# A hybrid diffusion trunk step in fp32: the second layer's up product by seven block products of 320 columns, and tokens in slabs without padding columns

## The chip, the core and the metric

The kernel runs on one core of a Trainium2 chip. The metric is the device time of the program in microseconds, the median of the runs; lower is better. The core has TensorE (PE, matmul), VectorE (DVE), ScalarE (ACT), GpSimd (POOL) and a queue of its own for DMA (SP). PEld is the loading of weights into TensorE, which overlaps its matmuls.

## The reference

One step of a trunk of two layers for 640 tokens: 128 context tokens and 512 latent ones, 1024 features. Per layer, cut to what matters:

```python
h = modulate(x, sh1, sc1)                       # RMS norm, scale, shift
proj = h @ p['w_in']                            # q, k, v, z, x/B/C, dt, two gates
attn = block_attention(q, k_all, v_all)
xbc = silu(dw_conv(xbc, conv_w, conv_b))        # 3 taps over tokens
ssd, h_final = ssd_branch(xbc, z, dt_raw, ...)  # scan in both directions
merged = sigmoid(ga) * (attn @ w_attn_o) + sigmoid(gs) * (ssd @ w_ssd_o)
x = x + g1 * (merged @ p['w_out'])
h = modulate(x, sh2, sc2)
u = dw_conv(h @ p['w_up'], p['ffn_conv_w'], p['ffn_conv_b'])   # 1024 -> 5632
u_val, u_gate = split(u, 2)
x = x + g2 * ((silu(u_gate) * u_val) @ p['w_down'])            # 2816 -> 1024
```

Everything is float32. The convolutions run over the tokens of one request, so context and latent tokens must not mix at their border.

## The kernel before

**Products in two parts.** A float32 operand is split into a high part (`wh` of the weights, `hT[0]` of the tokens, by a cast on ScalarE to fp32r) and a low part (`wl`, `hT[1]`, by `dve.tensor_sub` of the source and the high part). A product is three matmuls per block of 128 features: high by high, high by low, low by high. Weights come from DRAM into `wr` (two buffers of [128, 2048], 1 MB), and `wprep` makes `wh` and `wl` of them (three buffers each); `AHEAD = 2` units are recorded before the item that needs them.

**Feature-major products** (`feat_half`) have 128 weight columns stationary and tokens moving. They make x, B, C and dt of the input projection (25 feature blocks in each layer) and the up product (44 in each layer). The tokens lie with two columns of zeros between context and latent, 642 in all, and move in two parts of `HALF = (386, 256)` columns; one part is 8 blocks x 3 = 24 matmuls into one PSUM bank. `conv_in` brings it out twice on ScalarE (a copy into `raw`, the middle tap with its bias into `cc`), `conv_taps` adds the two outer taps on VectorE.

**Token-major products** (`tok_major`) have tokens stationary and 512 weight columns moving: 24 matmuls per tile of 128 tokens. The output projection (`w_out_item`) and the down product (`down_item`) are of this kind.

**The up stage.** `up_item(p, jl)` takes two weight units of 256 columns, one of the value half and one of the gate half: two feature blocks each, and two token parts, so 8 x 24 = 192 matmuls. After the convolution the gate block goes through `silu2` and the product with the value block and is split into `S["g", p]`. A layer has 11 items: four, then the down product of those 8 blocks in two items (`n`), four, down, three, down. The first item takes the first token parts of all four blocks ahead of the second parts, because the last tiles are still being normed: `w_out_item` with `n == 1` updates the five token tiles one by one and norms each (`norm_tile`, `norm_mod`), which splits it into `S["h2"]`, made by `new_hT`.

**What sets the order.** The program is recorded as operations on tiles (`Flow.record`) and then ordered by a list scheduler (`Flow.issue`) with costs of its own, ranks by class (`RANK`) and buffers granted in the order of asking. Each engine then runs its instructions strictly in that order. All are issued from one helper line, so rows of the profile tell by tile names what they are: `pf`, `pp`, `p`, `pq` are PSUM banks (`pf` three), `slab` holds tokens or gated blocks, `fw` the taps and biases of the up product's convolution, `tmp` the convolution's buffers (seven of class `f`, seven of class `d`).

## Time and profile before

| | us |
|---|---|
| median of 3 runs | 2858.25 (2858.05 to 2859.9) |
| span of the profiled execution | 2854.8 |
| TensorE busy | 2816.5 |
| VectorE busy | 2066.4 |
| ScalarE busy | 1291.9 |
| GpSimd busy | 90.5 |

The span runs from the first to the last instruction of the one execution that the hardware profiler recorded; 3.45 us separate it from the median. Busy times of one engine can overlap in themselves, since an instruction's recorded end lies behind the start of the next, so the pitch, from start to start, is read from the timeline. The second layer's up and down stage runs from 2384 us to the end.

### The profile page before, as it was taken

How to read it: one execution, taken by the hardware profiler on the slowest of the kernel's cores; microseconds unless marked ns; L12 is line 12 of the kernel's file. 1: busy time of each engine (PE TensorE's matmuls, PEld its weight loads, DVE VectorE, ACT ScalarE, POOL GpSimd, SP SyncE). 2: the span in 40 equal slices, each digit the busy share in tenths (PEclk: the TensorE clock that was granted, in tenths of full speed). 3: DMA queues.
4: the chain of work that ended last, by engine and by line, in shares of the span. 5: the costliest groups of instructions: out<-in, count | busy, mean ns of one | idle time of the engine just before them, and what ended most of it. 6: DMA issues, size and time to landing. Idle time of an engine off the chain costs nothing.

```text
span 2854.8 us, 41191 instructions
## 1 busy us (share of the span) xinstructions
PE 2816.5 (99%) x15620; PEld 2456.6 (86%) x15620; DVE 2066.4 (72%) x2851; ACT 1291.9 (45%) x2255; POOL 90.5 (3%) x408
## 2 busy tenths in 40 slices
PE   6999999999999999999999999999999999999999
PEld 4898997877788898998979989887887888989898
DVE  7878775987799599997677666598779456545554
ACT  6454654445353453452444645544454325524342
POOL 1200000000000000000011000000000000000000
PEclk9999999999999999999999999999999999999999
DMA  7343444677868546455352223457667553252423
GB/s 262 100 125 126 126 151 143 225 247 245 275 219 275 180 136 215 167 175 180 98 168 85 94 95 100 155 199 251 220 235 258 203 175 132 86 166 65 155 84 111
DMA packets 309679, 478.45 MB, mean 168 GB/s; under 512 B 19808, under 2 KB 139792, under 8 KB 304360
## 3 DMA queue, kind: packets, MB, share of 16 engines
q1 hardware_dynamic: 309480, 475.81, 50.0%
q8 instruction: 123, 2.02, 0.3%
q14 instruction: 76, 0.62, 0.1%
HBM read 384.08 MB, written 91.65 MB: 167 GB/s over the span
## 4 chain that ended last, share of the span: by engine, by line
PE 95%; DMA 3%; DVE 1%; ACT 1%; issue 0%; SPq 0%; POOL 0%; DVEq 0%; ACTq 0%
PE pf L178 79%; PE p L178 10%; PE pp L178 4%; PE pq L178 1%; DMA tmp<-in_state_ssd_dram 1%; DMA slab<-in_w_mod_dram 0%; DVE tmp L178 0%; DMA ga<-tmp 0%; DVE wl L178 0%; DMA tmp<-in_x_prompt_dram 0%; ACT tmp L178 0%; SPq L178 0%; DMA slab<-in_q_norm_dram 0%; DVE slab L178 0%; ACT wh L178 0%
## 5 line engine op out<-in xcount | busy, mean ns | idle before, releaser
L178 PE MATMUL pf<-wh,slab 128*128 128x512 f32 x3920 | 1268.3, 400 | 5.9 <-ACT slab L178 2.5
L178 PE MATMUL pf<-slab,wh 128*128 128x256 f32 (+1 forms) x4416 | 980.2, 311 | 3.4 <-DVE slab L178 1.9
L178 PEld LDWEIGHTS pf<-wh,slab 128*128 128x128 f32 x3920 | 733.1, 189 | 174.4 <-issue 7.3
L178 PE MATMUL pf<-wl,slab 128*128 128x512 f32 x1960 | 780.7, 398 | 0.0
L178 PEld LDWEIGHTS pf<-slab,wh 128*128 128x128 f32 x4416 | 741.8, 189 | 12.0 <-issue 5.7
L178 PE MATMUL pf<-slab,wl 128*128 128x256 f32 (+1 forms) x2208 | 685.1, 310 | 0.0
L178 DVE TENSOR_TENSOR wl<-wr,wh 128x2048 fp32r<-128x2048 f32 (+1 forms) x156 | 350.7, 2248 | 145.3 <-ACT wh L178 144.5
L178 PEld LDWEIGHTS pf<-wl,slab 128*128 128x128 f32 x1960 | 369.5, 189 | 86.6 <-issue 6.0
L178 ACT CAST wh<-wr 128x2048 fp32r<-128x2048 f32 (+1 forms) x156 | 293.0, 1879 | 320.7 <-PE pf L178 302.4
L178 PEld LDWEIGHTS pf<-slab,wl 128*128 128x128 f32 x2208 | 415.9, 188 | 3.0 <-issue 0.2
L178 DVE SCALAR_TENSOR_TENSOR tmp<-tmp,fw,tmp 128x642 f32<-128x642 f32 x176 | 155.5, 885 | 80.5 <-ACT tmp L178 66.3
L178 PE MATMUL p<-tmp,slab 128*128 128x64 f32 (+1 forms) x976 | 209.8, 336 | 0.3 <-DVE tmp L178 0.3
L178 ACT ACTIVATE tmp<-tmp 128x642 f32<-128x642 f32 (+2 forms) x176 | 120.9, 687 | 179.1 <-DVE tmp L178 145.5
L178 ACT ACTIVATE tmp<-pf,fw 128x386 f32<-128x386 f32 (+1 forms) x176 | 109.0, 620 | 175.4 <-PE pf L178 172.2
L178 DVE TENSOR_TENSOR tmp<-pf,tmp 128x512 f32<-128x512 f32 x100 | 68.3, 688 | 132.1 <-PE pf L178 131.8
L178 PEld LDWEIGHTS p<-tmp,slab 128*128 128x128 f32 x976 | 136.0, 190 | 16.2 <-ACT tmp L178 4.6
L178 ACT COPY tmp<-pf 128x256 f32<-128x256 f32 (+3 forms) x296 | 127.5, 431 | 44.1 <-PE pf L178 43.7
L178 DVE TENSOR_TENSOR slab<-tmp,slab 128x512 fp32r<-128x512 f32 (+4 forms) x182 | 109.0, 634 | 42.9 <-ACT slab L178 42.7
L178 DVE SCALAR_TENSOR_TENSOR macc<-tmp,cT,macc 128x512 f32<-128x512 f32 x196 | 137.7, 743 | 1.2 <-DMA tmp<-in_w_mod_dram 1.2
L178 DVE TENSOR_TENSOR tmp<-tmp,tmp 128x512 f32<-128x512 f32 (+3 forms) x190 | 133.7, 705 | 3.0 <-DMA tmp<-sz 0.6
L178 PEld LDWEIGHTS p<-cst,tmp 128*128 128x128 f32 (+2 forms) x750 | 92.3, 141 | 40.6 <-issue 16.1
L178 PE MATMUL p<-cst,tmp 128*128 128x128 f32 (+2 forms) x750 | 121.0, 276 | 5.1 <-DMA tmp<-in_state_ssd_dram 4.4
(131 smaller groups left out, 2564.3 us busy)
## 6 DMA issues: line engine op xcount, KB each, us to landing
wr<-in_w_in_dram SPq DMA_DIRECT2D x60, 1024.0 KB
wr<-in_w_up_dram SPq DMA_DIRECT2D x44, 1024.0 KB
slab<-row SPq DMA_DIRECT2D x40, 1024.0 KB
tmp<-in_w_mod_dram SPq DMA_DIRECT2D x116, 256.0 KB
tmp<-xres SPq DMA_DIRECT2D x85, 256.0 KB
wr<-in_w_down_dram SPq DMA_DIRECT2D x20, 1024.0 KB
tmp<-xs SPq DMA_DIRECT2D x72, 256.0 KB
xres<-tmp SPq DMA_DIRECT2D x70, 256.0 KB
```

The costliest lines, as they stand in the source:

```text
L178: self.ops.append((lane, lambda: call(*args, **kw), self._cost(lane, fn, outs, ins, kw), deps, touched, self.cls))
```

## The change

Four things are edited together.

1. **Up product of the second layer, all items but the first.** Of each weight unit (1024 x 256) the two feature blocks and the two halves of the 1024 inputs make four blocks `a11, a12, a21, a22` of 512 x 128; the tokens make four of 512 x 320. Their product is made by Winograd's form of Strassen's algorithm: seven block products of 12 matmuls of 320 columns (`product`), with sums of weights (`Sums`: s1 to s4, made in place in `wr`), sums of tokens (`Blocks.sums`: t1 to t4) and sums of products. Products accumulate on one another in a PSUM bank where they can; `win_unit` copies intermediate sums out between two accumulations. Of the last product of a unit (`rest`) the recording is put off into the next unit.
2. **No padding columns among the tokens.** `HALF = (256, 384)`; the context is tokens 0 to 127 at once, and `padded` puts the columns of a bank to their places when they leave it. `conv_bufs` clears the two border columns of `raw` and `cc` on GpSimd. The second layer's `S["h2"]` is a `Blocks`, in halves of 320.
3. **Slabs of one size.** One tag of four slabs for tokens instead of two tags of two; `NSLABD` 7 instead of 5. The decay tables of `dt_item` (`karr`) lie in one of these instead of in buffers of their own.
4. A rank `u` ahead of all others on ScalarE and VectorE for what empties PSUM in `win_unit`; a smaller scratch for GpSimd's DMA, which the kernel does not use.

```diff
-HALF = (386, 256)
-HOFF = (0, 386)
+HALF = (256, 384)
-NSLABD = 5
+NSLABD = 7
+WIN = (1,)
+TH = 320
...
-        "pe": {"m": 0, "d": 1, "f": 2}, "act": {"f": 0, "d": 1, "m": 2}, "dve": {"f": 0, "d": 1, "m": 2},
+        "pe": {"m": 0, "d": 1, "f": 2}, "act": {"u": -1, "f": 0, "d": 1, "m": 2},
+        "dve": {"u": -1, "f": 0, "d": 1, "m": 2},
...
+    class Blocks:
+        def __init__(self):
+            self.R = [slabd([P, 4, TOK]) for _ in range(2)]
+            self.X = {k: slab([P, 2, 4, TH], F32R) for k in ("11", "21", "22")}
+            self.X["12"] = slabd([P, 2, 4, TH], F32R)
...
+        def part(self, k, src=None):
+            x = self.X[k]
+            split(x[:, 0], x[:, 1], self.raw(k) if src is None else src)
+
+        def sums(self):
+            tr = slabd([P, 2, 4, TH])
+            for k in ("t1", "t2", "t3"):
+                self.X[k] = slabd([P, 2, 4, TH], F32R)
+            self.X["t4"] = slab([P, 2, 4, TH], F32R)
+            dve.tensor_sub(tr[:, 0], self.raw("11"), self.raw("12"))
+            self.part("t1", tr[:, 0])
+            dve.scalar_tensor_tensor(tr[:, 1], tr[:, 0], -1.0, self.raw("22"), ALU.mult, ALU.subtract)
+            self.part("t2", tr[:, 1])
+            t3, t4 = self.raw("12"), self.raw("21")
+            dve.tensor_sub(t3, self.raw("22"), t3)
+            self.part("t3", t3)
+            dve.scalar_tensor_tensor(t4, tr[:, 1], -1.0, t4, ALU.mult, ALU.subtract)
+            self.part("t4", t4)
...
+    class Sums:
+        def __init__(self, parts):
+            r, _ = wraw(parts, False)
+            v = r.rearrange("p (j k i c) -> p j k i c", j=2, k=4, i=2)
+            hl = [[flow.tile(wp, [P, 4, 4, P], F32R, n, nm(n), 3) for n in ("wh", "wl")] for _ in range(2)]
...
+            a11, a12, a21, a22 = v[:, 0, :, 0], v[:, 1, :, 0], v[:, 0, :, 1], v[:, 1, :, 1]
...
+            dve.tensor_add(s3, a11, a21)
+            put(0, 0, 2, v[:, :, :, 0])
+            dve.tensor_add(a21, a21, a22)
+            put(0, 2, 1, a21)
+            dve.tensor_add(a11, s3, a22)
+            put(0, 3, 1, a11)
+            dve.tensor_add(a12, a11, a12)
+            put(1, 0, 1, a12)
+            put(1, 1, 1, s3)
+            put(1, 2, 1, a22)
...
+    def product(ps, w, x, start):
+        wh, wl = w
+        for k in range(4):
+            for j, (w, b) in enumerate(((wh, 0), (wh, 1), (wl, 0))):
+                pe.matmul(
+                    ps, lhsT=w[:, k, :], rhs=x[:, b, k, :], start=start and k + j == 0, stop=k + j == 5,
+                    skip_group_check=not start,
+                )
...
+    def win_unit(W, X, bufs, taps, done):
...
+        product(a, W["a11"], X["11"], True)
+        now(act.copy, p1c, a)
+        product(c, W["s1"], X["t1"], True)
+        now(act.copy, p5c, c)
+        catch_up()
+        product(a, W["s2"], X["t2"], False)
+        now(act.copy, u2, a)
+        product(b, W["a12"], X["21"], True)
+        r0, c0 = bufs(0)
+        for src, dst in halves(r0):
+            now(dve.tensor_add, dst, p1c[:, src], b[:, src])
+        product(c, W["s4"], X["22"], False)
+        now(dve.tensor_add, r0[:, TH + 3:COLS + 1], u2, c)
+        product(a, W["s3"], X["t3"], False)
+        now(act.copy, u3, a)
+        conv(0, r0, c0)
+
+        def rest():
+            product(a, W["a22"], X["t4"], False)
+            r1, c1 = bufs(1)
+            dve.scalar_tensor_tensor(r1[:, TH + 3:COLS + 1], u3, -1.0, p5c, ALU.mult, ALU.subtract)
+            for src, dst in halves(r1):
+                now(act.mul, dst, a[:, src], -1.0)
+            conv(1, r1, c1)
+
+        behind.append(rest)
...
+        pool.memset(raw[:, P + 1:P + 3], 0.0)
+        pool.memset(cc[:, P:P + 2], 0.0)
...
-                    S["h2"] = new_hT()
+                    S["h2"] = Blocks() if l in WIN else new_hT()
...
+                        if l in WIN and i == 2:
+                            S["h2"].part("11")
+                            S["h2"].part("21")
+                if l in WIN and n == 1:
+                    S["h2"].part("12")
+                    S["h2"].part("22")
+                    S["h2"].sums()
...
-                add([w_feat(w_up, l, P * j, 256), w_feat(w_up, l, P * (NFF + j), 256)], up_item(p, jl))
+                us = [w_feat(w_up, l, P * j, 256), w_feat(w_up, l, P * (NFF + j), 256)]
+                if l in WIN and p + jl > 0:
+                    us = [lambda u=u: Sums(u) for u in us]
+                add(us, up_item(p, jl))
```

**Where instructions stand, TensorE, an up item of the second layer.** Before, at the step from a token part of 386 columns to the next of 256 (one feature block, `pf` the bank, `slab` the tokens):

```order
L178 MATMUL pf_3731<-slab_3653,wl_3702 128x386
L178 MATMUL pf_3731<-slab_3653,wh_3701 128x386
L178 MATMUL pf_3731<-slab_3655,wh_3701 128x386
L178 MATMUL pf_3731<-slab_3653,wl_3702 128x386
L178 MATMUL pf_3731<-slab_3653,wh_3701 128x386
L178 MATMUL pf_3731<-slab_3655,wh_3701 128x386
L178 MATMUL pf_3731<-slab_3653,wl_3702 128x386
L178 MATMUL pf_3732<-slab_3654,wh_3701 128x256
L178 MATMUL pf_3732<-slab_3656,wh_3701 128x256
```

Now, at the step from the first product of a unit (a11 by its tokens) to the second (s1 by the sum t1):

```order
L180 MATMUL pf_3765<-slab_3647,wl_3733 128x320
L180 MATMUL pf_3765<-slab_3647,wh_3732 128x320 x2
L180 MATMUL pf_3765<-slab_3647,wl_3733 128x320
L180 MATMUL pf_3765<-slab_3647,wh_3732 128x320 x2
L180 MATMUL pf_3765<-slab_3647,wl_3733 128x320
L180 MATMUL pf_3765<-slab_3647,wh_3732 128x320 x2
L180 MATMUL pf_3765<-slab_3647,wl_3733 128x320
L180 MATMUL pf_3766<-slab_3692,wh_3732 128x320 x2
L180 MATMUL pf_3766<-slab_3692,wl_3733 128x320
L180 MATMUL pf_3766<-slab_3692,wh_3732 128x320 x2
```

What moved: a bank is filled by 12 matmuls of 320 columns instead of 24, and the next product takes other weights of the same unit and other tokens.

**VectorE, the same items.** Before, one item's rows (`wl` a weight unit's low part, rows with `fw` the taps, the others gate, product and split):

```order
L178 TENSOR_TENSOR wl_3747<-wr_3745,wh_3746 128x2048
L178 SCALAR_TENSOR_TENSOR tmp_3738<-tmp_3737,fw_2252,tmp_3738 128x642 x2
L178 TENSOR_TENSOR wl_3750<-wr_3748,wh_3749 128x2048
L178 SCALAR_TENSOR_TENSOR tmp_3742<-tmp_3741,fw_2252,tmp_3742 128x642 x2
L178 SCALAR_TENSOR_TENSOR tmp_3742<-tmp_3741,tmp_3742 128x642
L178 SCALAR_TENSOR_TENSOR tmp_3752<-tmp_3751,fw_2252,tmp_3752 128x642
L178 TENSOR_TENSOR tmp_3742<-tmp_3742,tmp_3738 128x642
L178 SCALAR_TENSOR_TENSOR tmp_3752<-tmp_3751,fw_2252,tmp_3752 128x642
L178 TENSOR_TENSOR slab_3705<-tmp_3742,slab_3703 128x642
```

Now, a third of an item (`wr` rows are sums of weights in place, `wl` their low parts):

```order
L180 TENSOR_TENSOR wr_3731<-wr_3731 128x4x128
L180 TENSOR_TENSOR wl_3733<-wr_3731,wh_3732 128x512
L180 TENSOR_TENSOR wl_3735<-wr_3731,wh_3734 128x512
L180 SCALAR_TENSOR_TENSOR tmp_3750<-tmp_3749,fw_2248,tmp_3750 128x642
L180 TENSOR_TENSOR wl_3735<-wr_3731,wh_3734 128x512
L180 SCALAR_TENSOR_TENSOR tmp_3750<-tmp_3749,fw_2248,tmp_3750 128x642
L180 SCALAR_TENSOR_TENSOR tmp_3752<-tmp_3751,fw_2248,tmp_3752 128x642
L180 TENSOR_TENSOR tmp_3758<-wr_3753 128x512
L180 SCALAR_TENSOR_TENSOR tmp_3752<-tmp_3751,fw_2248,tmp_3752 128x642
L180 TENSOR_TENSOR wr_3753<-wr_3753 128x4x128
L180 TENSOR_TENSOR wl_3755<-wr_3753,wh_3754 128x1024
L180 SCALAR_TENSOR_TENSOR tmp_3752<-tmp_3751,tmp_3752 128x642
```

What moved: the low part of a unit of 2048 columns has become ten instructions, and they stand between the taps.

**VectorE, where the second layer's last token tile is modulated** (`TENSOR_SCALAR`, four blocks). Before, what follows is the tile's split, then the first item's taps:

```order
L178 TENSOR_SCALAR tmp_3691<-p_3592_3696,sm_3627 128x128 x4
L178 TENSOR_TENSOR slab_3656<-tmp_3692,slab_3654 128x4x128
L178 TENSOR_TENSOR slab_3656<-tmp_3691,slab_3654 128x4x128
L178 SCALAR_TENSOR_TENSOR tmp_3708<-tmp_3707,fw_2252,tmp_3708 128x642 x2
L178 SCALAR_TENSOR_TENSOR tmp_3711<-tmp_3710,fw_2252,tmp_3711 128x642 x2
L178 TENSOR_TENSOR wl_3725<-wr_3723,wh_3724 128x2048
```

Now the low parts and sums of whole blocks of 1280 columns follow (`slab_3645` and `slab_3646` are the tokens unsplit), then the rest of a weight unit:

```order
L180 TENSOR_SCALAR slab_3646<-p_3586_3690,sm_3619 128x128 x4
L180 TENSOR_TENSOR slab_3691<-slab_3645 128x1280
L180 TENSOR_TENSOR slab_3650<-slab_3645,slab_3650 128x1280
L180 TENSOR_TENSOR slab_3649<-slab_3646,slab_3649 128x1280
L180 TENSOR_TENSOR slab_3692<-slab_3691,slab_3692 128x1280
L180 SCALAR_TENSOR_TENSOR slab_3691<-slab_3691,slab_3646 128x1280
L180 TENSOR_TENSOR slab_3645<-slab_3646,slab_3645 128x4x320
L180 SCALAR_TENSOR_TENSOR slab_3646<-slab_3691,slab_3646 128x4x320
L180 TENSOR_TENSOR slab_3693<-slab_3691,slab_3693 128x1280
L180 TENSOR_TENSOR slab_3694<-slab_3645,slab_3694 128x1280
L180 TENSOR_TENSOR slab_3695<-slab_3646,slab_3695 128x1280
L180 TENSOR_TENSOR wl_3703<-wr_3699,wh_3702 128x512
```

What moved: ten instructions of 1280 columns stand between the last tile and the taps of the first item, which come third after the last row shown.

## Rows read from the trace of the kernel before

**Rows 1.** Page, part 1: busy us, share of the span, instructions.
```profile
PE 2816.5 (99%) x15620; PEld 2456.6 (86%) x15620; DVE 2066.4 (72%) x2851; ACT 1291.9 (45%) x2255; POOL 90.5 (3%) x408
```

**Rows 2.** Stretches: length, busy us of PE, PEld, DVE, ACT, POOL, clock, DMA.
```profile
2440.28:2468.23 27.95, 27.95 (x194) 27.95 (x193) 16.31 (x16) 14.07 (x23) 0.51 (x8) 1.00 0.23 76
1048.00:1076.00 28.00, 28.00 (x190) 27.46 (x190) 26.57 (x35) 14.69 (x24) 0.71 (x8) 1.00 0.46 150
```

**Rows 3.** Timeline of PE, an up item: start us, us, what, xcount, idle before.
```profile
2400.39 0.34 PE L178 MATMUL pf<-slab,wl 128*128 128x386 f32 x1
...
2406.23 0.34 PE L178 MATMUL pf<-slab,wl 128*128 128x386 f32 x1
...
2406.64 0.28 PE L178 MATMUL pf<-slab,wl 128*128 128x256 f32 x1
...
2407.66 0.28 PE L178 MATMUL pf<-slab,wl 128*128 128x256 f32 x1
```

**Rows 4.** Timeline of PE where attention's 320 columns stand.
```profile
160.38 1.04 PE L178 MATMUL pp<-slab,slab 128*128 128x320 f32 x6
161.26 0.33 PE L178 MATMUL pf<-slab,wh 128*128 128x386 f32 x1
```

**Rows 5.** Groups of DVE by shape: xcount, busy us, mean ns of one.
```profile
L178 DVE SCALAR_TENSOR_TENSOR tmp<-tmp,fw,tmp 128x642 f32<-128x642 f32 x176 | 155.5, 885 | 80.5 <-ACT tmp L178 66.3 <-issue 6.6 <-POOL tmp L178 2.5
...
L178 DVE TENSOR_TENSOR slab<-tmp,slab 128x512 fp32r<-128x512 f32 x100 | 64.8, 686 | 27.7 <-ACT slab L178 27.6
...
L178 DVE TENSOR_TENSOR tmp<-tmp,slab 128x128 f32<-128x128 f32 x64 | 14.3, 285 | 0.0
...
L178 DVE SCALAR_TENSOR_TENSOR tmp<-tmp,tmp 128x320 f32<-128x320 f32 x18 | 8.8, 491 | 0.5
L178 DVE TENSOR_TENSOR wl<-wr,wh 128x1024 fp32r<-128x1024 f32 x6 | 7.3, 1224 | 6.7 <-ACT wh L178 6.7
```

**Rows 6.** Timeline of DVE, second layer, without a wait between.
```profile
2385.35 1.29 DVE L178 TENSOR_TENSOR slab<-tmp,slab 128x512 fp32r<-128x512 f32 x2
...
2418.82 0.82 DVE L178 SCALAR_TENSOR_TENSOR tmp<-tmp,tmp 128x642 f32<-128x642 f32 x1
2419.55 0.88 DVE L178 SCALAR_TENSOR_TENSOR tmp<-tmp,fw,tmp 128x642 f32<-128x642 f32 x1
2420.35 0.82 DVE L178 TENSOR_TENSOR tmp<-tmp,tmp 128x642 f32<-128x642 f32 x1
```

**Rows 7.** Timeline of PE, second layer, output projection into up.
```profile
2382.82 0.39 PE L178 MATMUL pf<-wl,slab 128*128 128x512 f32 x1
...
2383.51 0.39 PE L178 MATMUL pf<-wl,slab 128*128 128x512 f32 x1
2384.64 0.59 PE L178 MATMUL pf<-slab,wh 128*128 128x386 f32 x2 [0.74 <-ACT slab L178]
2386.18 0.42 PE L178 MATMUL pf<-slab,wh 128*128 128x386 f32 x1 [0.94 <-DVE slab L178]
...
2387.27 0.53 PE L178 MATMUL pf<-slab,wl 128*128 128x386 f32 x1
...
2388.23 0.53 PE L178 MATMUL pf<-slab,wl 128*128 128x386 f32 x1
```

**Rows 8.** The same step of the first layer, PE, then DVE.
```profile
979.80 0.59 PE L178 MATMUL pf<-slab,wh 128*128 128x386 f32 x2 [0.73 <-ACT slab L178]
981.34 0.41 PE L178 MATMUL pf<-slab,wh 128*128 128x386 f32 x1 [0.95 <-DVE slab L178]
981.59 0.34 PE L178 MATMUL pf<-slab,wl 128*128 128x386 f32 x1
...
982.13 0.34 PE L178 MATMUL pf<-slab,wl 128*128 128x386 f32 x1
...
991.35 1.06 PE L178 MATMUL p<-cst,tmp 128*128 128x128 f32 x8
...
994.21 1.29 DVE L178 TENSOR_TENSOR slab<-tmp,slab 128x512 fp32r<-128x512 f32 x2 [0.38 <-ACT slab L178]
```

More of the change, by code (lines that the diff above doesn't have):

```diff
@@ L366, in nm, with slab @@
         return f"{s}_{uid[0]}"
-    def slab(h, shape, dt=F32):
-        return flow.tile(slabs, shape, dt, f"slab{h}", nm("slab"), 2)
+    def slab(shape, dt=F32):
+        return flow.tile(slabs, shape, dt, "slab", nm("slab"), 4)
     def slabd(shape, dt=F32):
@@ new lines, in product, with halves, catch_up @@
+    def product(ps, w, x, start):
[6 more added lines that the diff above has]
+                )
+    def halves(raw):
+        return (slice(0, P), raw[:, 1:P + 1]), (slice(P, TH), raw[:, P + 3:TH + 3])
+    behind = []
+    def catch_up():
+        while behind:
+            behind.pop(0)()
@@ new lines, in win_unit, with now, conv @@
+    def win_unit(W, X, bufs, taps, done):
+        W, X = W.w, X.X
+        a, c = psf()[:, 0:TH], psf()[:, 0:TH]
+        flow.cls = "d"
+        ta, tb = cv((P, 2, TH)), cv((P, 2, TH))
+        b = flow.tile(p1, [P, 512], F32, "p1", nm("p1"), 2)[:, 0:TH]
+        flow.cls = "f"
+        p1c, p5c, u2, u3 = ta[:, 0], ta[:, 1], tb[:, 0], tb[:, 1]
+        def now(fn, *args, **kw):
+            flow.cls = "u"
+            fn(*args, **kw)
+            flow.cls = "f"
+        def conv(k, raw, cc):
+            w0, w1, w2, bias = taps(k)
+            act.activation(cc, raw[:, 1:COLS + 1], AF.Identity, scale=w1, bias=bias)
+            conv_taps(raw, cc, w0, w2)
+            done(k)
+        product(a, W["a11"], X["11"], True)
[22 more added lines that the diff above has]
+        behind.append(rest)
@@ L597, in norm_mod @@
                 dve.tensor_scalar(h[:, k, :], src[:, k, :], sc, sh, ALU.mult, ALU.add)
-        b, o = part(i)
-        ks = slice(4 * n, 4 * n + 4)
-        split(hT[0][b][:, ks, o:o + P], hT[1][b][:, ks, o:o + P], h)
+        if not isinstance(hT, Blocks):
+            o = slice(i * P, (i + 1) * P)
+            split(hT[0][n][:, :, o], hT[1][n][:, :, o], h)
     def norm_tile(x0, x1, t, i, modT, hT):
@@ L972, in arr @@
                 return t2()[:, 0:n]
+            kar = slabd([P, 5, NT, 64])
+            kn = iter(range(5))
             def karr(tag):
-                return keep([P, NT, 64], F32, tag)
+                return kar[:, next(kn)]
             def fl(t):
@@ L1345, in half, with gated, new @@
                     raw, cc = bufs[a, s]
[L1346 to L1347 removed]
+                    if l in WIN:
+                        ps = feat_half(ws[s], 256, a * P, S["h2"].cols(h), TH)
+                        if h == 0:
+                            for src, dst in halves(raw):
+                                act.copy(dst, ps[:, src])
+                        else:
+                            act.copy(raw[:, TH + 3:COLS + 1], ps)
+                            act.activation(
+                                cc, raw[:, 1:COLS + 1], AF.Identity, scale=f[:, 1, s, j:j + 1], bias=f[:, 3, s, j:j + 1]
+                            )
+                    else:
+                        ps = feat_half(ws[s], 256, a * P, part_h(S["h2"], h), HALF[h])
+                        conv_in(raw, cc, ps, h, f[:, 1, s, j:j + 1], f[:, 3, s, j:j + 1])
                     if h == 1:
                         conv_taps(raw, cc, f[:, 0, s, j:j + 1], f[:, 2, s, j:j + 1])
[L1350 removed]
+                        gated(a, s)
+                def gated(a, s):
+                    if s == 1:
                         k = jl + a
[L1352 removed]
+                        (raw, cc), cu = bufs[a, 1], bufs[a, 0][1]
                         silu2(raw, cc)
                         dve.tensor_mul(cc, cc, cu)
[L1355 removed]
+                        split(gs[0][k // 4][:, k % 4, :], gs[1][k // 4][:, k % 4, :], cc)
+                def new(a, s):
+                    bufs[a, s] = conv_bufs()
+                    return bufs[a, s]
+                if isinstance(ws[0], Sums):
+                    for s in range(2):
+                        win_unit(
+                            ws[s], S["h2"], lambda a, s=s: new(a, s),
+                            lambda a, s=s: [f[:, r, s, j0 + a:j0 + a + 1] for r in range(4)],
+                            lambda a, s=s: gated(a, s),
+                        )
+                    return
                 if p == 0 and jl == 0:
@@ L1369, in fn @@
             def fn(ws):
+                catch_up()
                 g = gate_bc(l, 1, n)
```

74 lines of the change are left out of this document (46 added, 28 removed).

## Prediction

> **What bounds the kernel now.** I read the busy times first. TensorE is busy for 2816.5 us of a span of 2854.8 us, and all matmuls together leave it 38 us idle [rows 1]. So the time is the length of TensorE's stream, and an edit gains what it takes out of that stream, less what TensorE then waits. VectorE is second with 2066.4 us, but that is a mean over stages. The stage that the change rebuilds is the second layer's up product, so I read one of its items next, in the table of stretches: 27.95 us, TensorE busy all of it, VectorE 16.31 us, ScalarE 14.07 us [rows 2]. The engine that can take the bound from TensorE there is VectorE, which gets the new sums.
>
> **The price of a matmul.** TensorE's busy time overlaps, so I take start to start. Eleven times three matmuls of 386 columns go from 2400.39 to 2406.23, which is 0.177 us each; nine of 256 columns go from 2406.64 to 2407.66, 0.113 us each [rows 3]. 96 x (0.177 + 0.113) = 27.8 us, the item of [rows 2]. Six of 320 columns start at 160.38 and the next matmul at 161.26, 0.147 us each [rows 4]; by columns between 256 and 386 it would be 0.145. I take 0.146.
>
> **Term 1, seven products for eight.** Before, a pair of feature blocks (one weight unit) is two blocks of 24 matmuls of 386 and 24 of 256 columns, half an item: 13.98 us. After, it is seven products of 12 matmuls of 320 columns, as the order of TensorE shows, 84 x 0.146 = 12.26 us. That is 1.72 us for each of 20 units, **-34.3 us** (-32.6 at 0.147, -36.0 at 0.145). The first item of the second layer stays a product by eight; its 192 matmuls of 320 columns take 28.0 us, as before.
>
> **Term 2, no padding columns.** 94 feature blocks (25 of the input projection in each layer, 44 of the first layer's up) have 24 matmuls each of 384 instead of 386 columns: 2,256. The trace has no 384. From the nearest row, 386, in proportion, one saves 0.0009 us, together 2 us. On the line through 256 (0.113) and 512 columns (0.230: the third of one three starts at 2382.82 and that of the next at 2383.51 [rows 7]), 384 would take 0.1715 and one saves 0.0055, together 12 us. I take the nearest, **-2 us**, and keep 12 for the range.
>
> **Term 3, what VectorE has to do.** Its price is start to start too: two of 512 columns last 1.29 us together, where one lasts 0.686 [rows 5, 6]; one of 0.82 us is followed after 0.73, one of 0.88 after 0.80 [rows 6]. So an instruction in a full queue costs its duration less 0.086 us. With the durations of [rows 5] this makes 0.60 for 512 columns, 1.14 for 1024, 0.80 for a tap of the convolution, 0.74 for 642 columns without a per-partition scalar [rows 6], 0.405 for 320, 0.20 for 128; between these 0.27 for 192, and beyond them, at 1.053 ns a column, 1.41 for 1280 and 2.2 for 2048.
>
> A weight unit before was one subtraction of 2048 columns, 2.2 us. Now it is four additions of 512, one low part of 1024 and five of 512: 9 x 0.60 + 1.14 = 6.5 us. Joining the products adds 0.20 + 0.27 + 2 x 0.405 = 1.3 us a unit. Eight taps (6.4) and six instructions of 642 columns (4.4) an item stay. So an item asks VectorE for 2 x 7.8 + 10.8 = 26.4 us, beside 24.5 us of TensorE: VectorE no longer hides behind the item, though 26.4 is still below the 27.95 of before. It can only work ahead and behind: the down products between are long and ask it for little.
>
> So I count VectorE's rows in the order of the changed kernel over each of the three stretches, up products and the head of the down products that needs them, against TensorE's. After the last token tile is modulated the first stretch has 147 instructions: 10 of 1280 (the token sums), 49 of 512, 5 of 1024, 32 taps, 24 of 642, 12 of 320, 6 of 192, 6 of 128, 3 of 2048, together 106.9 us, and 1.7 us before they begin. TensorE has 628 matmuls of 320 columns and 63 of 512 at 0.230 before it needs the last gated tile: 91.7 + 14.5 = 106.2 us. The second stretch: 161 instructions, 106.1 us and 1.5 before, against 98.1 + 14.5 = 112.6. The third: 117 instructions, 77.3 and 1.5, against 73.6 + 10.4 = 84.0. With no gap on VectorE TensorE would wait 2.4 us in all. Gaps there will be: nearly every low part waits for ScalarE's high part, and the joins wait for TensorE while everything behind them on VectorE stands. How dense can VectorE be while TensorE is fed? In an up item of the first layer it was busy 26.57 of 28.00 us, 95%, and TensorE lost nothing [rows 2], but a part of that was modulation work that could wait. At 95% the three stretches cost 8.0 + 0.6 + 0 = 8.6 us, at 90% 14.3 + 6.8 + 3.4 = 24.5 us. I take 93%: 10.4 + 3.0 + 0.6 = **+14 us**.
>
> **Term 4, the first layer's step into up.** The first halves now need two tiles instead of three, so the waits of 0.73 and 0.95 us for the third [rows 8] go. But four first halves last 4 x 24 x 0.113 = 10.9 us instead of 17.0, and the last tile's split ends only at 994.21 + 1.29 = 995.5 [rows 8]. TensorE leaves the output projection at about 979.1; with 10.9, two groups of transposes (0.8 each) and eight small matmuls (0.23) it is done at 993.4 and then waits some 1.5 us, with a chance of a slower clock: after 1.7 us of such waits in the second layer the 386-column matmuls start 0.32 us apart from 2387.27 to 2388.23 instead of 0.177 [rows 7], which is the 1.2 GHz level and costs 1 to 2 us in the few that it lasts, while after the same waits in the first layer three take 0.54 us from 981.59 on [rows 8]. **+1 us**, from -1 to +4.
>
> At no cost I enter the additional memsets of the two padding columns (POOL is busy 90.5 us in all [rows 1]), ScalarE (14.07 us of an item [rows 2]; the casts grow from 2048 to 3584 columns a unit, still under 24.5), and the two more slabs, since a freer order elsewhere can only win back idle time, of which little is left [rows 1].
>
> **Sum.** -34.3 - 2 + 14 + 1 = -21.3 us. The profiled execution spans 2854.8 us and the median is 2858.25, 3.45 us around it; the sum goes on both alike: a span of 2833.5, a median of **2837 us**.
>
> [...] The rows of a full queue [rows 6] show an instruction of VectorE starting 0.086 us before the one ahead has ended. [...]
>
> **Rivals.** (a) VectorE keeps up, waits of 3 us or less, and 384 columns run nearer the line: -36 - 12 + 2.4 = about -46, 2812; with 2 us for the padding 2824. For it speaks that the second and third stretch have 5 us in hand, against it that the first has none. (b) Full durations: 0.086 us more for 147, 161 and 117 instructions makes 119.5, 119.9 and 87.4 us, waits of 15.0 + 8.8 + 4.9 = 28.7 us and -6.6 in all, 2852. For it speaks that instructions which wait for their own predecessor do not overlap, against it the queue without waits [rows 6]. (c) **Slower**: VectorE becomes the bound of the up items. Its queue is strictly in order, and a join that waits for a product holds the weights of the next unit behind it, for which TensorE then waits. It decides from a density of 87%: there the waits are 18.4 + 10.9 + 6.4 = 35.7 us and eat the gain. At 84% they are 22.8 + 15.2 + 9.5 = 47.5 us, +12, 2870. For it speaks that an item of before, with idle time to spare, filled VectorE to 58% only [rows 2] and so proves nothing of 90; against it the 95% of the first layer. (d) The change does not do what it says: the order has seven products of 12 in each unit, so this is left at 0.01.
>
> **How the numbers follow.** My forecast, waits of 3 to 25 us (2825 to 2848): 0.50. (a), below 2825: 0.14. (b), 2848 to 2856: 0.13. Between (b) and (c), 2856 to 2864: 0.06. (c), above 2864: 0.16, and (d) 0.01. About 0.2% (5.7 us) is what a measurement of this kernel can tell from no change: faster than 2852.5 is the forecast, (a) and a small part of (b), 0.68; within it 0.15; slower 0.17. The range leaves out the far end of (a) and the worse half of (c), a density below 85% (43.4 us of waits, +8): 2814 to 2866.
>
> **What would show it.** TensorE's instructions fall by 240 and its 320-column matmuls start 0.145 to 0.147 us apart. VectorE's busy time rises by about 20 x 5.6 us and 11 for the token sums, to 2190 us. An item of seven products takes 24.5 us where it is not held. TensorE's waits for the low parts of weights and for the joins stand in the first of the three stretches above all, 14 us in the three, and VectorE is busy over 90% there. 384-column matmuls 0.172 us apart would say that term 2 was too small; up items of over 27 us with VectorE near 85% and TensorE waiting for it would say (c); full queues of VectorE without overlap, (b).

## The result, and the profile after

The changed kernel takes 2875.27 us (median of 4 runs, 2872.91 to 2878.35) against 2859.07 of the kernel before in the same comparison: a ratio of 1.0062, 95% interval 1.0049 to 1.0074. It is slower by 16 us, where 21 us of gain were predicted. The profiled execution spans 2871.1 us, 16.3 more than before.

Part 1 of the page of the changed kernel, busy us of each engine (before: [rows 1]):

```profile
PE 2804.9 (98%) x15380; PEld 2426.5 (85%) x15380; DVE 2184.4 (76%) x3113; ACT 1331.4 (46%) x2353; POOL 111.2 (4%) x672
```

TensorE has 240 instructions fewer and is busy 11.6 us less. VectorE's busy time rose to 2184.4, as forecast (2190). The edit does what it says, and yet the span grew, so TensorE idles more, somewhere. To find where, I cut both timelines of TensorE at the same steps of the program: the first matmul of 512 columns after the convolutions, the first of an up product, and so on.

| stage (start read from TensorE's timeline) | before | after | difference |
|---|---|---|---|
| until the first layer's z product | 402.7 | 402.4 | -0.3 |
| first layer: z, gates, SSD, output projection | 577.1 | 603.4 | **+26.3** |
| first layer: up and down | 549.2 | 552.2 | +3.0 |
| second layer: input projection, attention | 291.3 | 291.0 | -0.3 |
| second layer: z, gates, SSD, output projection | 564.3 | 566.1 | +1.8 |
| second layer: up and down | 470.2 | 456.0 | **-14.2** |

The last row is the place of the change, and it gains. The second is a stage in which nothing was rebuilt, a layer ahead of the block products, and it loses more. Its start in the timeline of TensorE before (its end there, 979.80, is in [rows 8]), then its two ends in the changed kernel's:

```profile
402.72 0.48 PE L178 MATMUL pf<-wh,slab 128*128 128x512 f32 x1
```

```profile
402.38 0.48 PE L180 MATMUL pf<-wh,slab 128*128 128x512 f32 x1
...
1005.82 0.40 PE L180 MATMUL pf<-slab,wh 128*128 128x256 f32 x2
```

In that stage two things share TensorE: token-major products (16 items of 5 x 24 matmuls of 512 columns) and SSD, 20 chunks (four groups of heads, five token tiles each), each a chain over VectorE, ScalarE and TensorE. Of the 1920 matmuls of the items, 1440 need nothing of SSD's last group. The last two items with SSD's output need it, tile by tile, and the two of the output projection come behind them. Both kernels at the end of SSD, in stretches (length, busy us of PE, PEld, DVE, ACT, POOL, granted clock, DMA), first before:

```profile
800.00:840.00 40.00, 40.00 (x205) 32.29 (x203) 37.69 (x53) 20.65 (x41) 0.00 (x0) 1.00 0.58 202
840.00:880.00 40.00, 40.00 (x193) 32.96 (x192) 36.03 (x56) 16.12 (x29) 1.37 (x2) 1.00 0.83 285
880.00:920.00 40.00, 40.00 (x192) 32.86 (x191) 35.85 (x53) 12.65 (x17) 0.23 (x2) 1.00 0.77 244
```

and after:

```profile
800.00:840.00 40.00, 39.86 (x184) 31.42 (x184) 29.65 (x40) 20.57 (x40) 0.00 (x0) 1.00 0.75 276
840.00:880.00 40.00, 35.58 (x162) 25.77 (x162) 39.03 (x57) 20.62 (x39) 0.00 (x0) 0.90 0.58 191
880.00:920.00 40.00, 32.88 (x149) 26.23 (x148) 34.77 (x54) 12.69 (x21) 1.38 (x2) 0.89 0.74 245
```

Before, TensorE is full to the last. After, from 840 to 880 VectorE is full (39.03 of 40) and TensorE runs beside it with 162 matmuls where it had 193, then with 149 where it had 192. The output of the last SSD chunk (eight heads, `p`, 64 columns, 16 matmuls), before at 847.86 us:

```profile
847.86 1.90 PE L178 MATMUL p<-tmp,slab 128*128 128x64 f32 x16
```

and after, that of the last two chunks (872.77 and 882.06 us), with what stands around it on TensorE:

```profile
872.77 2.00 PE L180 MATMUL p<-tmp,slab 128*128 128x64 f32 x16 [0.72 <-ACT tmp L180]
874.58 0.48 PE L180 MATMUL pp<-tmp,slab 128*128 128x512 f32 x1
876.40 1.22 PE L180 MATMUL pp<-tmp,slab 128*128 128x512 f32 x2 [1.34 <-DVE tmp L180]
877.42 1.05 PE L180 MATMUL pf<-wh,slab 128*128 128x512 f32 x2
878.27 0.63 PE L180 MATMUL pf<-wl,slab 128*128 128x512 f32 x1
...
882.06 1.90 PE L180 MATMUL p<-tmp,slab 128*128 128x64 f32 x16
...
893.86 0.40 PE L180 MATMUL pf<-wl,slab 128*128 128x512 f32 x1
901.33 1.22 PE L180 MATMUL pf<-wh,slab 128*128 128x512 f32 x2 [7.07 <-DVE tmp L180]
```

The last output comes 34 us later. By 860 us the 1440 matmuls, and the 24 of the first token tile that SSD had finished, were used up, so the last chunks ran with little beside them, each step waiting for the one before on another engine. Two matmuls of 512 columns take 0.85 us (877.42 to 878.27) instead of 0.46: the lower level of the clock, after TensorE had waited again and again. Then a token-major product waits 7.07 us. The engine named, VectorE, holds the join that frees a bank, but does modulation (`macc`) meanwhile; what it stands behind is on ScalarE's row, the load of SSD's last output (`y`) from DRAM, and on its own, the load of the join's other operand (`pb`), which the DMA queue issues right after that of `y` (895.47 and 895.94 us). The modulation lasts until 899.35 itself, so these rows do not tell what an earlier load alone would have saved. VectorE, then ScalarE:

```profile
891.98 7.37 DVE L180 SCALAR_TENSOR_TENSOR macc<-tmp,cT,macc 128x512 f32<-128x512 f32 x11
...
900.58 0.69 DVE L180 TENSOR_TENSOR tmp<-pf,tmp 128x512 f32<-128x512 f32 x1 [0.39 <-DMA tmp<-pb]
901.19 0.74 DVE L180 SCALAR_TENSOR_TENSOR macc<-tmp,cT,macc 128x512 f32<-128x512 f32 x1
```

```profile
898.85 0.62 ACT L180 CAST slab<-tmp 128x512 fp32r<-128x512 f32 x1 [8.30 <-DMA tmp<-y]
```

None of this is new work: the stage has the same 1920 matmuls in another order. TensorE's waits in it sum to 15.0 us, against 3.8 before, and by the granted clock of the last two stretches (0.90 and 0.89) some 8 us more went to the lower level; the rest of the 26 us is spread. Whether the order is the cause is for the experiments.

### The profile page after: what moved, and what is told of

Same layout as the page of the kernel before. It is cut to its first block, busy times and chain, and to the rows that moved or that the text cites. A ratio compares the mean times of both kernels' runs of the same rounds, so it can differ in the third digit from the quotient of the medians.

```text
span 2871.1 us, 41287 instructions
## 1 busy us (share of the span) xinstructions
PE 2804.9 (98%) x15380; PEld 2426.5 (85%) x15380; DVE 2184.4 (76%) x3113; ACT 1331.4 (46%) x2353; POOL 111.2 (4%) x672
## 5 line engine op out<-in xcount | busy, mean ns | idle before, releaser
L180 PE MATMUL pf<-slab,wh 128*128 128x256 f32 (+2 forms) x4096 | 918.4, 311 | 0.8 <-ACT tmp L180 0.7
L180 PEld LDWEIGHTS pf<-slab,wh 128*128 128x128 f32 x4096 | 687.9, 188 | 10.0 <-ACT tmp L180 1.6
L180 PE MATMUL pf<-slab,wl 128*128 128x256 f32 (+2 forms) x2048 | 636.9, 311 | 3.8 <-DVE wl L180 3.8
L180 ACT CAST wh<-wr 128x2048 fp32r<-128x2048 f32 (+2 forms) x236 | 323.7, 1379 | 342.8 <-PE pf L180 306.5
L180 DVE TENSOR_TENSOR wl<-wr,wh 128x2048 fp32r<-128x2048 f32 (+2 forms) x236 | 382.0, 1628 | 98.1 <-ACT wh L180 97.8
L180 PEld LDWEIGHTS pf<-slab,wl 128*128 128x128 f32 x2048 | 385.5, 188 | 8.1 <-DVE wl L180 5.0
L180 DVE TENSOR_TENSOR slab<-slab,slab 128x512 f32<-128x512 f32 (+2 forms) x137 | 119.7, 895 | 45.0 <-ACT slab L180 41.4
L180 ACT COPY tmp<-pf 128x384 f32<-128x384 f32 (+6 forms) x300 | 126.9, 430 | 49.1 <-PE pf L180 48.5
L180 ACT ACTIVATE tmp<-pf 128x512 f32<-128x512 f32 (+3 forms) x150 | 73.5, 504 | 153.8 <-PE pf L180 140.3
L180 DVE TENSOR_TENSOR tmp<-tmp,slab 128x512 f32<-128x512 f32 (+3 forms) x254 | 122.5, 516 | 5.9 <-DMA tmp<-xs 4.7
```

Source lines behind the costliest of these rows:

```text
L180: self.ops.append((lane, lambda: call(*args, **kw), self._cost(lane, fn, outs, ins, kw), deps, touched, self.cls))
```

## The experiments

There are two theories. **Order**: the list scheduler places the first layer's SSD later in the changed program, because small shifts tip its choices; the loss of 26 us has nothing to do with the block products. **Buffers**: the decay tables in a slab, slabs of one size or the block products hold SSD back. For each kernel I counted, in the order of TensorE, how many of the token-major matmuls stand ahead of the last chunk's output: 1396 before, 1470 after: all of the 1440 that could have covered it, and 30 of the items that need SSD's last group.

**Block products away.**

```diff
-WIN = (1,)
+WIN = ()
```

> The changed kernel with the second layer's up product as a product by eight again, tokens without padding, slabs of one size and the parts of 256 and 384 columns kept. Before, the first layer's stage of z, gates, SSD and output projection lasts from 402.7 to 979.8 us; with the change from 402.4 to 1005.8, 26.3 us more. Theory (the order): the loss there has nothing to do with the block products, so the stage stays at 603 us, the second layer's up and down stage goes back from 456 to about 470 us, and the time is 2875 + 14 = 2889 us. Rival (the block products' buffers or rank reach into the first layer): the stage goes back to 577 us and the time to 2859 to 2863 us. Both have the 384 columns: if they cost nothing or gain nothing, the first layer's up and down stage stays at 549 to 552 us.

Measured: 2887.39 us, ratio to before 1.0108 (1.0089 to 1.0128). The stage lasts from 403.0 to 1004.3, 601.3 us; the second layer's up and down 472 us. The loss is there without the block products, which gain 12 us by the medians and 14.1 by the spans.

**Only the widths of the token parts**, in the kernel before.

```diff
-HALF = (386, 256)
-HOFF = (0, 386)
+HALF = (258, 384)
+HOFF = (0, 258)
```

(and the two lines that say which tile lies in which part)

> The kernel before, with one edit: the token parts are 258 columns (context, first latent tile and the padding) and then 384, instead of 386 and then 256. Slabs, padding, tables and the up product are those of before. Theory (the order): the work is the same, but the list scheduler puts the first layer's SSD later: in its order 1488 token-major matmuls stand before the output of the last SSD chunk, where 1440 can go without it; before there were 1396, with the change 1470. So the stage lasts about 603 us instead of 577 and the time is 2859 + 26 = 2885 us. Rival (decay tables in a slab and slabs of one size hold SSD back): neither is in this kernel, 2859 us. The pitch of 384 columns from slabs of their own is read beside it: 0.1715 us by the line through 256 and 512 columns, 0.1733 as in the changed kernel, where the 256-column matmuls went from 0.113 to 0.118 us.

Measured: 2886.48 us, ratio 1.0099 (1.0081 to 1.0117). Of the 16 matmuls of SSD's last output, 14 start from 879.70 us on:

```profile
405.94 0.48 PE L178 MATMUL pf<-wh,slab 128*128 128x512 f32 x1
...
879.70 1.67 PE L178 MATMUL p<-tmp,slab 128*128 128x64 f32 x14
...
1001.95 0.40 PE L178 MATMUL pf<-slab,wh 128*128 128x258 f32 x2
```

The stage takes 596.0 us, 19 of the 26 lost, with the tables, the padding and the two tags of slabs of before. The rest of the 28 us by which its span is longer is spread (3 us ahead of the stage, 2.5 and 3.6 in the two up and down stages). Buffers are not needed for the loss. That leaves the widths themselves as a rival; the next run has the widths of before too.

**Nothing but two constants of the scheduler**, in the kernel before.

```diff
-        "pe": {"pe": 0.0, "act": 197.0, "dve": 197.0, "pool": 197.0, "dma": 200.0},
+        "pe": {"pe": 0.0, "act": 220.0, "dve": 220.0, "pool": 197.0, "dma": 200.0},
```

> The kernel before, with nothing changed but two constants of its list scheduler: the delay that it assumes from TensorE to ScalarE and to VectorE is 220 instead of 197 ns. Every instruction is the same, only the order is another. Theory (the order): the order of before was a favourable one that small shifts lose; here 1476 token-major matmuls stand before the output of the last SSD chunk of the first layer, so that stage lasts some 20 to 26 us more and the time is 2879 to 2885 us. Rival (the part widths themselves cost the time, by what they do on the engines): 2859 us, within 3.

Measured: 2873.25 us, ratio 1.0058 (1.0039 to 1.0076). The stage takes 601.1 us (398.7 to 999.8) and SSD's last output begins at 873.98. The loss of the change, 24 us of it in the same stage, comes without any instruction changed. The total was less than expected since this order wins 4 us ahead of the stage and 2 us in each up and down stage.

**Other constants in the changed kernel.**

```diff
-        "pe": {"pe": 0.0, "act": 197.0, "dve": 197.0, ...
-        "act": {"pe": 160.0, "act": 153.0, "dve": 141.0, ...
-        "dve": {"pe": 160.0, "act": 130.0, ...
-        "dma": {"pe": 1200.0, "act": 1200.0, "dve": 1200.0, ...
-                    heapq.heappush(slots[x.tag], x.end + 150.0)
+        "pe": {"pe": 0.0, "act": 215.0, "dve": 215.0, ...
+        "act": {"pe": 160.0, "act": 153.0, "dve": 150.0, ...
+        "dve": {"pe": 160.0, "act": 150.0, ...
+        "dma": {"pe": 1000.0, "act": 1000.0, "dve": 1000.0, ...
+                    heapq.heappush(slots[x.tag], x.end + 50.0)
```

> The changed kernel, with nothing changed but constants of its list scheduler (delays assumed from TensorE to ScalarE and VectorE 215, ScalarE to VectorE 150, VectorE to ScalarE 150, from a DMA 1000, and a buffer free 50 ns after its last use instead of 150). Every instruction is the same. Theory (the order): 1409 token-major matmuls stand before the output of the last SSD chunk of the first layer, as in the kernel before (1396) and not as in the changed one (1470), so the stage goes back to some 577 us and the time to 2875 - 26 = 2849 us, 10 us under the kernel before. Rival (the slabs, the padding or GpSimd's memsets cost the time): 2875 us.

Measured: 2854.16 us, ratio 0.9987 (0.9978 to 0.9997): 21 us less than the changed kernel, with the same instructions. The stage takes 581.8 us (396.99 to 978.82) and SSD's last output begins at 849.88. Stage and time are 5 us above what was expected; with slabs in another place (plan_aligned, below) the stage takes 576.4. For the loss in this stage the rival falls; the slabs come back below with a loss of their own.

**Are these constants simply better?** They went into the kernel before too.

> The kernel before with the planner constants of after_plan: every instruction as before, another order. 1390 token-major matmuls stand before the output of the last SSD chunk of the first layer; before it was 1396. Theory (its own order was a favourable one already): 2855 to 2862 us, nothing gained. Rival (these constants make any kernel faster, so that what plan_aligned gained of the order isn't what the change had lost): 2845 us or less.

Measured: 2868.19 us, ratio 1.0033 (1.0020 to 1.0047), outside both expectations. The first layer's stage is as the count says (579.7 us, SSD's last output from 849.7), but the second layer's z to output projection takes 572 instead of 564.3 us. The constants are not better; they give another order, good in one stage and worse in another. The kernel before had a favourable one. With these constants in both kernels the change gains 14 us (2868.2 to 2854.2); with the old ones it loses 16. The sign of the result hangs on the order.

**Where the operands lie.** In the changed kernel 256-column matmuls stood further apart than before. The timeline of TensorE in a first-layer up item:

```profile
1060.91 0.28 PE L180 MATMUL pf<-slab,wl 128*128 128x256 f32 x1
...
1063.05 0.28 PE L180 MATMUL pf<-slab,wl 128*128 128x256 f32 x1
```

18 matmuls in 2.14 us, 0.119 each; before, 0.113 [rows 3]. In the built programs the token slabs begin at a multiple of 64 bytes in each partition before, and 32 bytes past one after, since a slab is 10,272 bytes. One edit sizes them to 10,304:

```diff
-            bm = slabd([P, 4, COLS], F32R)
+            bm = slabd([P, 4, PADW], F32R)
```

> The kernel of the run after_plan (changed kernel, other planner constants), with one edit: one of the tiles of the common slabs is asked for with rows of 644 instead of 642 columns, so a slab is 10,304 instead of 10,272 bytes in each partition. The order is the same instruction for instruction. In the built programs of the changed kernel and of after_plan the slabs that hold the tokens begin 32 bytes past a multiple of 64 in each partition, in the kernel before and in this one at a multiple of 64. Theory (place in memory): that is why the 256-column matmuls stand 0.118 us apart in the changed kernel and 0.1135 before, and 512-column ones 0.237 and 0.234; both go back here: 2,256 x 0.0048 = 11 us from the first, up to 13 us from some 4,700 of the second, a time of 2830 to 2843 us against 2854. Rival (it comes from longer rows in the slabs, or from the other work of these stages): the pitches stay and the time is 2854 us, within 3.

Measured: 2838.90 us, ratio to before 0.9937 (0.9921 to 0.9953): 15 us less than after_plan, and 18 us less than the kernel before. And the converse in the kernel before:

```diff
+    flow.tile(slabs, [P, 8], F32, "shift", nm("shift"), 1)
```

> The kernel before, with an unused tile of 32 bytes in each partition ahead of the slabs, so that every slab begins 32 bytes past a multiple of 64. Widths, rows and order are those of before. Theory (place in memory): 256-column matmuls go from 0.1135 to 0.118 us, 512-column ones from 0.234 to 0.237, 386-column ones may rise too, and the time by 11 to 25 us, 2869 to 2883. Rival (the longer rows of the slabs, or other work): 2858 us, within 3.

Measured: 2871.63 us, ratio 1.0049 (1.0031 to 1.0067), 15 us slower. Its 256-column matmuls, and those of plan_aligned:

```profile
1033.88 0.28 PE L178 MATMUL pf<-slab,wl 128*128 128x256 f32 x1
...
1034.59 0.28 PE L178 MATMUL pf<-slab,wl 128*128 128x256 f32 x1
```

```profile
1030.87 0.28 PE L180 MATMUL pf<-slab,wl 128*128 128x256 f32 x1
...
1031.56 0.28 PE L180 MATMUL pf<-slab,wl 128*128 128x256 f32 x1
```

Six matmuls in 0.71 and in 0.69 us, 0.118 and 0.115. The shifted kernel is at 0.118 throughout. In plan_aligned part of the items stand at 0.1135 (26 of 62 runs of 15 or more in a row) and part at 0.118, so the place in memory explains the time of both kernels, but not every row; what else decides a 256-column matmul is open. Both edits also shift the `tmp` buffers, which lie behind the slabs, by an odd multiple of 32 bytes. The matmuls whose pitch changed read only slabs and weight units, and the weight units begin at multiples of 64 bytes in all four kernels; whether the shifted `tmp` buffers have a share in the 15 us was not tested.

**The same edit alone in the changed kernel.**

> The changed kernel with one edit alone, the slabs of 10,304 instead of 10,272 bytes, so that they begin at a multiple of 64 bytes; its order is that of the changed kernel. plan_aligned against after_plan was 15 us faster, before_shift32 against the kernel before 15 us slower. Theory (place in memory and order add up): 2875 - 11 to 15 = 2860 to 2864 us, so that the order alone is worth the 21 to 25 us from here to plan_aligned's 2839. Rival (the first gain had to do with the other order): 2872 us or more.

Measured: 2863.32 us, ratio 1.0020 (1.0010 to 1.0029): 12 us less than the changed kernel. Its stage of SSD still takes 603 us. Alone, the order is worth 21.1 us (after_plan) and the place 12.0; together (plan_aligned) 36.4, so they add up within 3 us.

**What the block products are worth.**

> The kernel of the run after_plan with the second layer's up product as a product by eight again. The order of the first layer is the same as in after_plan. Theory: in no_blocks against the changed kernel the seven block products were worth 2887 - 2875 = 12 us; the same here, 2854 + 12 to 14 = 2866 to 2868 us, and the kernel before (2857 to 2858) is faster than this one by the slabs that begin 32 bytes off, with nothing gained by the padding. Rival (the blocks are worth what the prediction had, 20 us and more, and were masked by the order): 2874 us or more.

Measured: 2867.94 us, ratio 1.0037 (1.0024 to 1.0050). Against after_plan the blocks are worth 14 us, as in the first pair, and not 20.

**VectorE in the second layer.** Items of the changed kernel that start after a down stage, in stretches as above:

```profile
2583.10:2607.60 24.50, 24.50 (x169) 24.46 (x168) 18.54 (x31) 13.57 (x25) 0.54 (x8) 1.00 0.29 97
2607.60:2632.00 24.40, 24.00 (x164) 23.70 (x163) 23.65 (x38) 15.99 (x31) 0.81 (x12) 1.00 0.26 87
2632.00:2656.50 24.50, 24.02 (x162) 23.50 (x161) 24.23 (x39) 15.59 (x30) 0.97 (x15) 1.00 0.26 88
```

An item takes 24.4 to 24.5 us. VectorE, which could work ahead during the down products, is at 18.5 us in the first item and at 24.2 in the third. The edit leaves the four additions of each unit out, so that the products take other blocks in place of the sums and the second layer's up product is no longer the right one:

```diff
-            dve.tensor_add(s3, a11, a21)
+            s3 = a21
...
-            dve.tensor_add(a21, a21, a22)
-            dve.tensor_add(a11, s3, a22)
-            dve.tensor_add(a12, a11, a12)
```

> The kernel of the run after_plan with the four additions of weight blocks of each unit left out (the seven products use other blocks in place of the sums, so the up product of the second layer is not the right one): VectorE has 4 x 0.6 = 2.4 us less in each of 20 units, TensorE the same matmuls. In the changed kernel an item that is not held takes 24.4 us and VectorE is busy for 23.65 and 24.23 of it, and TensorE waits 2 to 4.5 us at each step from up to down. Theory (VectorE, at 97 to 99% of an item, is what holds the second layer's stage): those waits go, 10 to 14 us, a time of 2840 to 2844 us. Rival (they are the length of the chain from the last product over convolution and gate to the split, not the amount of VectorE's work): 2851 to 2854 us.

Measured: 2829.01 us, ratio 0.9905 (0.9886 to 0.9923), 25 us less than after_plan, twice what was expected. The waits of TensorE in the second layer's up and down stage, first after_plan, then this kernel (us in all, times, longest):

```profile
PE pf L180 <- ACT slab L180: 8.8, 4, 3.1
PE pf L180 <- DVE wl L180: 3.1, 3, 2.2
PE p L180 <- DVE tmp L180: 0.5, 1, 0.5
PE pf L180 <- ACT tmp L180: 0.5, 1, 0.5
```

```profile
PE pf L180 <- ACT slab L180: 0.8, 1, 0.8
PE p L180 <- DVE tmp L180: 0.8, 2, 0.5
```

12.9 us of waits became 1.6. The stage became 437.4 instead of 458.8 us, 21.4 less, which is 10 more than the waits. Most of the rest is the clock behind them. Stretches of after_plan with a granted clock (third number from the right) under 1.00:

```profile
2390.80:2498.50 107.70, 104.91 (x701) 103.44 (x700) 100.78 (x145) 68.50 (x127) 8.71 (x65) 0.98 0.23 74
2498.50:2561.70 63.20, 60.05 (x255) 47.86 (x255) 40.30 (x54) 16.43 (x22) 0.91 (x13) 0.97 0.50 159
...
2664.50:2724.80 60.30, 57.01 (x233) 45.16 (x232) 35.94 (x48) 13.30 (x18) 0.91 (x13) 0.94 0.48 153
```

What they lack to 1.00, times their lengths, is 7 to 8 us; the other 2 to 3 us I cannot place. Without the additions the clock is 1.00 from 2390 to 2827 us. One such place in the changed kernel:

```profile
2833.49 1.61 PE L180 MATMUL pf<-wh,slab 128*128 128x512 f32 x4 [2.45 <-ACT slab L180]
2834.89 0.63 PE L180 MATMUL pf<-wl,slab 128*128 128x512 f32 x1
2835.32 0.63 PE L180 MATMUL pf<-wh,slab 128*128 128x512 f32 x1
...
2837.87 0.39 PE L180 MATMUL pf<-wl,slab 128*128 128x512 f32 x1
```

After a wait of 2.45 us seven matmuls start 0.43 us apart (2834.89 to 2837.87) instead of 0.23, the level of 1.2 GHz. So the amount of VectorE's work holds this stage, not the length of the chain from product to split, which the edit leaves as it was. For the 3.1 us of waits for `wl` the chain from a loaded weight to its low parts, which the edit shortens, is not excluded.

**The additions on GpSimd**, all four or two of them, in plan_aligned.

```diff
-            dve.tensor_add(s3, a11, a21)
+            pool.tensor_add(s3, a11, a21)
```

(and so for the others, or for a21 + a22 and a11 + a12 alone)

> plan_aligned with the four additions of weight blocks of each unit on GpSimd instead of VectorE (the planner takes 1.1 us for one). Leaving them out made after_plan 25 us faster. GpSimd is busy under 5% of the second layer's stage, but no row shows what an addition of 512 columns takes there: between VectorE's 0.65 us and four times that. Theory (VectorE's amount of work holds the stage, and GpSimd works beside it): 2839 - 12 to 22 = 2817 to 2827 us. Rival (an addition on GpSimd takes so long, over 2.5 us, that weights come late, or it slows VectorE's own instructions): 2839 us or more.

> As pool_sums, with two of the four additions on GpSimd (a21 + a22 and a11 + a12) and two on VectorE. If GpSimd's additions are cheap, half of the gain of pool_sums: 2839 - 6 to 11 = 2828 to 2833 us. If they are slow, over 2.5 us, two of them still fit into half an item of 12.2 us where four don't, and this one is the faster of the two: 2825 to 2833 us against 2839 and more.

Measured: 2856.62 us with four (ratio to before 1.0001, 0.9992 to 1.0011) and 2847.51 with two (0.9969, 0.9959 to 0.9979), against 2838.90 with none. Both were expected at 2833 us or less if GpSimd works beside VectorE; both are slower than no move at all. Groups by shape (busy us, mean ns of one), GpSimd with four additions (the two of a unit that stay in `wr`), then VectorE's low parts of 512 columns in the second layer's stage with four, with two and with none:

```profile
L180 POOL TENSOR_TENSOR wr<-wr 128x512 f32<-128x512 f32 x40 | 67.6, 1698 | 1.5
...
L180 DVE TENSOR_TENSOR wl<-wr,wh 128x512 fp32r<-128x512 f32 x80 | 80.6, 1023 | 8.9 <-ACT wh L180 7.8
```

```profile
L180 DVE TENSOR_TENSOR wl<-wr,wh 128x512 fp32r<-128x512 f32 x80 | 61.4, 779 | 12.0 <-ACT wh L180 12.0
```

```profile
L180 DVE TENSOR_TENSOR wl<-wr,wh 128x512 fp32r<-128x512 f32 x80 | 53.9, 684 | 7.2 <-ACT wh L180 7.2
```

An addition takes GpSimd 1.70 us, under the bound of 2.5 that I had set, but VectorE's own instruction went from 0.684 to 1.023 us: what VectorE was spared in additions it lost in its other work. In the second layer's up and down stage it is busy 380 us with four additions moved, 364 with two and 366 with none. The Trainium skill ("SBUF — State Buffer", section "Who interferes with whom") states that a VectorE instruction with two inputs in SBUF contends with a GpSimd instruction that reads SBUF. The rows agree.

## Why the prediction was wrong

**The step that failed** is the sentence at the end of the costs: "At no cost I enter ... the two more slabs, since a freer order elsewhere can only win back idle time". An order can also lose. All instructions are placed by one list scheduler, and the first layer's stage depends on how many products that can wait are still left while SSD ends. That was to be read before the run: the order of TensorE has 1396 of these products ahead of SSD's last output before and 1470 after. Over all fourteen kernels the count sorts the stage: those with 1390 to 1409 take 576 to 582 us in it, those with 1470 to 1488 take 596 to 603. I compared the order at the steps that the terms spoke of and not in the stage that the change only touched by its widths. It cost 26 us in that stage, and 21 to 24 us of the time (2875.3 - 2854.2 by after_plan, 2863.3 - 2838.9 by the two with aligned slabs).

**A cost not in the sum at all**: slabs that begin 32 bytes past a multiple of 64, 12 us in the changed kernel. The two make 33 to 36 of the 37.5 us between forecast and result. With both out of the way (plan_aligned) the change gains 18 us; that this is near the 21 of the forecast is in part luck, since term 2 was too small and the price in term 3 too small as well.

**Term 1**, seven products for eight, was right within a tenth. Items take 24.4 to 24.5 us as forecast. Where VectorE is relieved the stage takes 437.4 us against 470.2 before, 32.8 us less, with as much waiting in both (1.6 and 1.7 us). The lower clock of [rows 7] cost the kernel before some 1.7 us of that (0.83 granted from 2386 to 2396), so the term measures 31 to 33 us against the 34.3 of the sum.

**Term 3**, VectorE, was right in the sum of the waits and too small in its price. The forecast was +14 us of waits, the changed kernel has 14.1 in its second up and down stage:

```profile
PE pf L180 <- ACT slab L180: 9.4, 5, 3.0
PE pf L180 <- DVE wl L180: 3.8, 3, 3.0
PE pf L180 <- ACT tmp L180: 0.5, 1, 0.5
PE p L180 <- DVE tmp L180: 0.4, 1, 0.4
```

The sum is right in part by luck: the forecast had 10.4, 3.0 and 0.6 us in the three stretches, the trace has 5.7, 4.3 and 4.1, and the waits for the last gated block (`ACT slab`) stand in all three down stages.

And I priced a microsecond of waiting at a microsecond. The kernel before waits 1.7 us in this stage [rows 7], so the waits grew by 12.4 us; 34.3 - 12.4 is 21.9, and the stage gained 14.2. The lower clock behind the long waits costs the changed kernel about 3 us (0.93 in the stretch 2440 to 2465, 0.97 from 2817 on), the kernel before 1.7; the other 6 us of the difference I cannot place. I had shown the lower clock behind waits of 1.7 us in [rows 7] and used it for term 4 only.

**Term 2**, no padding columns. 384-column matmuls start 0.1735 us apart, near the line through 256 and 512 columns and not near the proportion: about 2,256 x 0.0035 = 8 us by [rows 3], not 2. It was not seen in the time, since the 256-column ones lost 0.005 each by the place of the slabs, 11 us.

**Term 4**, the first layer's step into up: TensorE waits 1.0 us there, 1.7 before. Within its range.

**The rivals.** The time came out slower, at the time of the slow rival (c), but not by it: (c) needed a stage that loses, and the stage of the block products gained 14 us. VectorE did become the bound there, without eating the gain. Rival (b), no overlap in VectorE's queue, is ruled out by the rows shown above: eleven instructions of `macc` take 7.37 us, where one lasts 0.74. In (a) the 2812 left out term 4; the sum gives 2814, which decides nothing. Nothing in my list had a loss outside the changed stage, so a range built from these cases could not hold the time.

## What to carry to other kernels

Where a scheduler or a planner orders the whole program, an edit of one stage is an edit of all: compare the order in the tightest stages first, above all how much work that can wait is left when a serial chain ends, and measure the edit once more under another order before judging it. Price a wait of TensorE with the lower clock behind it; here 11 us of waits went with 21 us of time, some 7 of it the clock's. After an edit of buffer sizes, look at where the operands begin.

## What the runs showed of the hardware that was not expected

- The start of TensorE's operands in SBUF matters: token slabs 32 bytes past a multiple of 64 go with 12 to 15 us of 2857 in three pairs of kernels (after_aligned, plan_aligned, before_shift32), in which the `tmp` buffers move too. 256-column matmuls went from 0.1135 to 0.118 us, 512-column ones with their stationary tokens in these slabs from 0.234 to 0.237 (medians over 60 and more runs of 15 or more in a row), though with the slabs at a multiple of 64 part of the 256-column ones stayed at 0.118. 384 and 320 columns showed nothing clear.
- GpSimd's additions slow VectorE: 512 columns with two inputs from 0.684 to 0.779 us with two of them a unit and to 1.023 with four.
- After waits of 2.2 to 3.1 us TensorE ran at its lower level for 3 us and more, in several places but not in all: behind the waits of 2.3 us at 2541.9 and 3.0 us at 2702.5 of the changed kernel the granted clock stayed at 1.00.
